# An mLSTM's running maxima: the DMAs that write and broadcast them are issued by GpSimd instead of ScalarE

## The chip, the cores and the metric

The kernel runs on one core of a Trainium2 chip. The metric is the device time of one execution in microseconds (us). The engines are TensorE (PE in the profile, its weight loads PEld), VectorE (DVE), ScalarE (ACT), GpSimd (POOL) and SyncE (SP). Each engine runs its own queue of instructions in order; a queue can hold DMA issues as well as computations, and an instruction that waits for a semaphore holds everything behind it in its queue.

## The reference

A two-layer decoder trunk for one sequence of 256 tokens, width 1024. Every layer is a half-step SwiGLU feed-forward, a token mixer beside four memory cross-attention heads, and a second half-step feed-forward. Layer 0 mixes tokens by an mLSTM (4 heads, head width 128 for keys, 256 for values), layer 1 by sliding-window attention. What matters here is the mLSTM's stabiliser. With `b` the running sum of the log forget gates and `i` the input gate,

```
b = jnp.cumsum(fc, axis=-1)
log_d = b[..., :, None] - b[..., None, :] + ic[..., None, :]
m_t = jnp.maximum(m_inter, jnp.max(log_d, axis=-1))
s = jnp.einsum('bhjd,bhsd->bhjs', qc, kc) * jnp.exp(log_d - m_t[..., None])
```

The kernel does this for all 256 tokens at once: with a[s] = i[s] - b[s] and g[t] = max over s up to t of a[s] (and 0), the weight of key s for query t is exp(a[s] - g[t]) under the causal mask. The running maxima g form 4 rows (heads) of 256 values. They are needed as rows that are the same on all 128 partitions, because keys lie on the partitions and queries along the free dimension.

## The kernel before, in words

Activations are kept transposed (features on partitions). Every weight tile of 128 x 1024 numbers is loaded by a DMA on SyncE's queue (tile `wr`, 5 buffers, L218), rounded on ScalarE to a high part (`wh`, 8 buffers, L211) and its rest formed on VectorE (`wl`, 8 buffers, L212); three matmuls per tile (L225 to L227) give nearly full precision. The rest goes through 8 PSUM banks.

The order of TensorE's and SyncE's instructions is fixed by a small planner (class `Weave`, L61): the main program yields after each group of matmuls, side chains (generators) are spawned with a delay, and each `yield` of a side chain says after how many estimated microseconds its next part may be placed. ScalarE, VectorE and GpSimd get their order from a scheduler that may move instructions.

In the mLSTM layer (`mixer_a`, L660) the gate columns are computed with the first query group of the cross-attention (L692 to L703). Then, side by side:

- `gates` (L711) transposes the gates to 4 rows (L714), forms log-sigmoids on ScalarE and VectorE (L716 to L723), runs the sum as a scan (L724), a = i - b (L725), the running maximum as a scan (`gg`, L726), b + g (L727) and its exp (`em`, L728, recorded at the helper's line L132). It then writes `gg` to a small HBM tensor `gd` (L729) and reads it back twice (L731), two heads at a time, each copy broadcast to all 128 partitions into a tile `gb[i]` of 128 x 512 numbers. TensorE's transposes of `av` and `em` into the columns `acol` (L736, L737) follow after a delay.
- `cross_spawn` (L579) normalises query rows (`head_norm`, with a power on GpSimd, L385), transposes them (L236), copies them with a gain to SBUF on ScalarE (L587, recorded at L132, input `bank,gqk`), and then each head does its scores (L599, recorded at L231), maxima (L602), exp (L605), reciprocal (L606) and normalisation (L607).
- `scores` (L747) uses `gb` first: VectorE subtracts the broadcast row from the mask (L752, L753), ScalarE takes exp with `acol` as bias, VectorE multiplies with the key-query products (L760).

Several helpers record all their operations at one line: matmuls of plain products at L231, transposes at L236, activations at L132.

Of the kernel before, what the change touches and what calls it, by code (L numbers as in the profile page):

```python
# [19 lines left out]
P = 128  # L20
# [78 lines left out]
def tile_trunk(ctx: ExitStack, tc: tile.TileContext, a, out):  # L99
    nc = tc.nc  # L100
# [30 lines left out]
    def act(*args, **kw):  # L131
        ins = nc.scalar.activation(*args, **kw)  # L132
        if args[2] not in (AF.Copy, AF.Square):
            tabled[0] = ins
# [6 lines left out]
    def unit(dt):  # L141
        return mk(up, [P, 2, T], dt, "u")
# [7 lines left out]
    def mo():  # L150
        return mk(pb8, [P, 512], F32, "bank")
# [82 lines left out]
    def transpose(ps, src):  # L234
        k = src.shape[0]
        nc.tensor.transpose(ps, src, ident[:k, :k])  # L236
        wv.now += 0.107
# [422 lines left out]
    def mixer_a(x, nxt):  # L660
# [44 lines left out]
        ipre, fpre, ab, bc, av, gg, em, one = (gt[i // 2][0:4, i % 2] for i in range(8))  # L705
        gd = a["gd"]
        gb = [unit(F32) for _ in range(2)]
# [3 lines left out]
        def gates():  # L711
            ps = mo()
            for h in range(2):
                transpose(ps[:36, h * P:(h + 1) * P], gts[:, h])  # L714
            nc.vector.memset(one, 1.0)
            nc.scalar.copy(ipre, ps[0:4, :T])  # L716
            nc.scalar.copy(fpre, ps[32:36, :T])
            nc.vector.tensor_scalar(ipre, ipre, gbias[:, 0:1], None, op0=ALU.add)
            nc.vector.tensor_scalar(fpre, fpre, gbias[:, 1:2], None, op0=ALU.add)
            nc.vector.scalar_tensor_tensor(out=ab, in0=fpre, scalar=-1.0, in1=fpre, op0=ALU.mult, op1=ALU.max)  # L720
            act(ab, ab, AF.Exp, scale=-1.0)
            act(ab, ab, AF.Ln, bias=1.0)
            nc.vector.scalar_tensor_tensor(out=fpre, in0=fpre, scalar=0.0, in1=ab, op0=ALU.min, op1=ALU.subtract)  # L723
            nc.vector.tensor_tensor_scan(bc, one, fpre, 0.0, ALU.mult, ALU.add)  # L724
            tt(out=av, in0=ipre, in1=bc, op=ALU.subtract)  # L725
            nc.vector.tensor_tensor_scan(gg, one, av, 0.0, ALU.mult, ALU.max)  # L726
            tt(out=em, in0=bc, in1=gg, op=ALU.add)  # L727
            act(em, em, AF.Exp, scale=-1.0)  # L728
            nc.scalar.dma_start(gd, gg)  # L729
            for i in range(2):  # L730
                nc.scalar.dma_start(gb[i], gd[2 * i:2 * i + 2, :].partition_broadcast(P))  # L731
            yield LAT['gates']
            pc = mo()
            for i, r in enumerate((av, em)):
                for h in range(2):
                    transpose(pc[:, (2 * i + h) * 4:(2 * i + h) * 4 + 4], r[:, h * P:(h + 1) * P])  # L736
            nc.vector.tensor_copy(acol, pc[:, :16])  # L737
            gated.append(True)

        wv.spawn(gates(), LAT['gate'])  # L740
        hsc = head_scales(x.rc, P, True)
        cross_spawn([p[:, 8:264] for p in gps], 0, 0, hsc, ys)
# [299 lines left out]
```

## Time and profile before

| | |
|---|---|
| time, median of 3 runs | 1015.86 us (1015.59 to 1018.35) |
| the profiled execution | 1016.86 us |
| its span, first to last instruction | 1015.1 us |
| mean granted TensorE clock | 0.997 |
| DMAs issued by ScalarE around 260 us | 3: `gd` at 259.07, the broadcasts from 261.26 |
| GpSimd, busy | 33.7 us, 3% of the span |

The page lists busy time per engine, a strip of 40 slices of the span (each about 25.4 us), the DMA queues, the chain of work that ended last, and the costliest groups. The views quoted below have these columns: the chain gives start, length, and what ran; a timeline gives start, length, engine, line, operation, output<-input, shapes and count, and in brackets the idle time before it with what ended that idle time; stretches give the busy time and count of PE, PEld, DVE, ACT and POOL, then the granted TensorE clock, the DMA share and GB/s. ACTq and POOLq are DMA issues of that engine's queue.

### The profile page before, as it was taken

How to read it: one execution, taken by the hardware profiler on the slowest of the kernel's cores; microseconds unless marked ns; L12 is line 12 of the kernel's file. 1: busy time of each engine (PE TensorE's matmuls, PEld its weight loads, DVE VectorE, ACT ScalarE, POOL GpSimd, SP SyncE). 2: the span in 40 equal slices, each digit the busy share in tenths (PEclk: the TensorE clock that was granted, in tenths of full speed). 3: DMA queues.
4: the chain of work that ended last, by engine and by line, in shares of the span. 5: the costliest groups of instructions: out<-in, count | busy, mean ns of one | idle time of the engine just before them, and what ended most of it. 6: DMA issues, size and time to landing. Idle time of an engine off the chain costs nothing.

```text
span 1015.1 us, 20581 instructions
## 1 busy us (share of the span) xinstructions
PE 999.3 (98%) x8572; PEld 980.4 (97%) x8572; DVE 653.7 (64%) x1060; ACT 520.1 (51%) x766; POOL 33.7 (3%) x32
## 2 busy tenths in 40 slices
PE   8999999999899999999999999999999999999998
PEld 7999999999799999999999999999987899999998
DVE  6866665566656676666567666656787766665551
ACT  7754545446466454444455544545557654444440
POOL 1200000001000000000000000000121000000000
PEclk9999999999899999999999999999999999999999
DMA  9776555666434566655566565566532246655550
GB/s 308 245 245 197 189 188 180 192 195 200 136 132 136 181 187 194 200 189 174 191 209 195 191 201 192 170 201 194 183 129 81 90 139 212 200 191 181 193 168 21
DMA packets 172180, 182.70 MB, mean 180 GB/s; under 512 B 6100, under 2 KB 167304, under 8 KB 172088
## 3 DMA queue, kind: packets, MB, share of 16 engines
q1 hardware_dynamic: 170848, 179.60, 55.5%
q10 hardware_dynamic: 1016, 1.58, 0.5%
q8 instruction: 67, 1.10, 0.4%
q0 software_dynamic: 224, 0.22, 0.2%
q14 instruction: 25, 0.20, 0.1%
HBM read 180.32 MB, written 1.05 MB: 179 GB/s over the span
## 4 chain that ended last, share of the span: by engine, by line
PE 91%; DVE 4%; ACT 2%; DMA 1%; POOL 1%; issue 1%; SPq 0%; ACTq 0%; DVEq 0%; POOLq 0%
PE bank L225 29%; PE bank L226 29%; PE bank L227 29%; PE bank L231 2%; ACT u L132 1%; DVE wl L212 1%; PE bank L236 1%; POOL col L385 1%; DMA wr<-in_mem_w_kv_dram 1%; DVE u L961 0%; DVE col L945 0%; PE bank L976 0%; DVE u L394 0%; DMA gd_dram<-u 0%; ACT wh L211 0%
## 5 line engine op out<-in xcount | busy, mean ns | idle before, releaser
L212 DVE TENSOR_TENSOR wl<-wr,wh 128x1024 fp32r<-128x1024 f32 (+1 forms) x348 | 414.7, 1193 | 281.9 <-ACT wh L211 281.3
L211 ACT CAST wh<-wr 128x1024 fp32r<-128x1024 f32 (+1 forms) x348 | 357.2, 1028 | 393.4 <-PE bank L226 369.2
L225 PE MATMUL bank<-xh,wh 128*128 128x256 f32 x1536 | 427.5, 278 | 0.0
L226 PE MATMUL bank<-xl,wh 128*128 128x256 f32 x1536 | 425.1, 277 | 0.0
L227 PE MATMUL bank<-xh,wl 128*128 128x256 f32 x1536 | 425.1, 277 | 0.0
L226 PEld LDWEIGHTS bank<-xl,wh 128*128 128x128 f32 x1536 | 289.3, 188 | 0.2
L225 PEld LDWEIGHTS bank<-xh,wh 128*128 128x128 f32 x1536 | 289.0, 188 | 0.2
L227 PEld LDWEIGHTS bank<-xh,wl 128*128 128x128 f32 x1536 | 288.9, 188 | 0.0
L225 PE MATMUL bank<-u,wh 128*128 128x256 f32 x896 | 249.3, 278 | 0.0
L226 PE MATMUL bank<-u,wh 128*128 128x256 f32 x896 | 247.6, 276 | 0.0
L227 PE MATMUL bank<-u,wl 128*128 128x256 f32 x896 | 247.6, 276 | 0.0
L225 PEld LDWEIGHTS bank<-u,wh 128*128 128x128 f32 x896 | 168.2, 188 | 1.9 <-issue 1.7
L226 PEld LDWEIGHTS bank<-u,wh 128*128 128x128 f32 x896 | 168.3, 188 | 0.1
L227 PEld LDWEIGHTS bank<-u,wl 128*128 128x128 f32 x896 | 168.2, 188 | 0.0
L225 PE MATMUL bank<-wh,xh 128*128 128x256 f32 (+1 forms) x208 | 60.0, 288 | 0.0
L226 PE MATMUL bank<-wl,xh 128*128 128x256 f32 (+1 forms) x208 | 58.1, 279 | 0.0
L227 PE MATMUL bank<-wh,xl 128*128 128x256 f32 (+1 forms) x208 | 58.0, 279 | 0.0
L487 DVE TENSOR_TENSOR t<-bank,rb 128x256 f32<-128x256 f32 x88 | 36.6, 420 | 7.3 <-PE bank L227 7.3
L225 PEld LDWEIGHTS bank<-wh,xh 128*128 128x128 f32 x208 | 39.1, 188 | 0.5 <-issue 0.3
L226 PEld LDWEIGHTS bank<-wl,xh 128*128 128x128 f32 x208 | 39.1, 188 | 0.1
L227 PEld LDWEIGHTS bank<-wh,xl 128*128 128x128 f32 x208 | 39.0, 187 | 0.0
L490 DVE TENSOR_TENSOR t<-t,bank 128x256 f32<-128x256 f32 x88 | 32.7, 412 | 1.8 <-ACT t L132 1.8
(167 smaller groups left out, 656.7 us busy)
## 6 DMA issues: line engine op xcount, KB each, us to landing
wr<-in_ffn_w_in_dram SPq DMA_DIRECT2D x176, 512.0 KB, 3.4
wr<-in_ffn_w_out_dram SPq DMA_DIRECT2D x80, 512.0 KB, 3.4
wr<-in_a_w_in_dram SPq DMA_DIRECT2D x26, 512.0 KB, 3.6
wr<-in_b_w_in_dram SPq DMA_DIRECT2D x14, 512.0 KB, 4.5
wr<-in_a_w_out_dram SPq DMA_DIRECT2D x12, 512.0 KB, 3.2
wr<-in_b_w_out_dram SPq DMA_DIRECT2D x12, 512.0 KB, 3.2
wr<-in_ffn_w_out_dram SPq DMA_DIRECT2D x16, 256.0 KB, 2.6
wr<-in_mem_w_kv_dram SPq DMA_DIRECT2D x7, 512.0 KB, 8.0
```

The costliest lines, as they stand in the source:

```text
L132: ins = nc.scalar.activation(*args, **kw)
L211: last[0] = nc.scalar.copy(hi[:, i * n:(i + 1) * n], src[:, i * n:(i + 1) * n])
L212: tt(out=lo[:, i * n:(i + 1) * n], in0=src[:, i * n:(i + 1) * n], in1=hi[:, i * n:(i + 1) * n].bitcast(F32), op=ALU.subtract)
L225: nc.tensor.matmul(ps, wh, xh, start=start, stop=False, skip_group_check=True)
L226: nc.tensor.matmul(ps, wh, xl, start=False, stop=False, skip_group_check=True)
L227: nc.tensor.matmul(ps, wl, xh, start=False, stop=stop, skip_group_check=True)
L231: nc.tensor.matmul(ps, lhsT, rhs, start=start, stop=stop, skip_group_check=True)
L236: nc.tensor.transpose(ps, src, ident[:k, :k])
L385: nc.gpsimd.tensor_tensor(out=u[:, 8:8 + 2 * n], in0=u[:, 0:2 * n], in1=mhalf[:, 0:2 * n], op=ALU.pow)
L487: tt(out=t[:, m], in0=ps[m][:, :T], in1=x.rb, op=ALU.mult)
L490: tt(out=t[:, m], in0=t[:, m], in1=ps[m][:, T:], op=ALU.mult)
```

## The change

The three DMAs of `gates` are issued from GpSimd's queue; nothing else in the source differs.

```diff
             tt(out=em, in0=bc, in1=gg, op=ALU.add)
             act(em, em, AF.Exp, scale=-1.0)
-            nc.scalar.dma_start(gd, gg)
+            nc.gpsimd.dma_start(gd, gg)
             for i in range(2):
-                nc.scalar.dma_start(gb[i], gd[2 * i:2 * i + 2, :].partition_broadcast(P))
+                nc.gpsimd.dma_start(gb[i], gd[2 * i:2 * i + 2, :].partition_broadcast(P))
             yield LAT['gates']
```

In the resulting queues they stand on GpSimd behind the second power of the cross-attention's query norm (L385) and ahead of the first power of the mLSTM's output norm (L251). On VectorE the scheduler puts the normalisation of the second query group (L394) and the scaling of the mLSTM's queries (L769) ahead of one weight split (L212), and the copy of `acol` (L737) ahead of a reciprocal (L606). TensorE's and SyncE's queues are unchanged.

## The prediction

> **What bounds the kernel now.** I read the page first, for the engine that fills the span.
>
> ```profile
> span 1015.1 us, 20581 instructions
> PE 999.3 (98%) x8572; PEld 980.4 (97%) x8572; DVE 653.7 (64%) x1060; ACT 520.1 (51%) x766; POOL 33.7 (3%) x32
> PEclk9999999999899999999999999999999999999999
> ```
>
> TensorE is busy for 98% of the span, so only time in which it stands still, or runs slowly, can be won. The clock row has one slice below 9, the eleventh, 254 to 279 us: that is where the changed DMAs are. Next I read the chain of waits there (start, length, what).
>
> ```profile
> 257.90 0.69 DVE u L726
> 259.07 2.17 DMA gd_dram<-u
> 261.26 0.36 ACTq L731
> 261.65 0.45 ACTq L731
> 262.14 0.70 ACT u L132
> 262.88 2.08 PE bank L231 x4
> 264.96 0.21 PE bank L225
> ...
> 267.52 1.37 PE bank L236 x8
> 268.89 1.09 PE bank L231 x4
> 269.98 0.12 PE bank L225
> ...
> 271.24 0.12 PE bank L227
> ```
>
> The scan (L726) makes the maxima; their write to HBM is on the chain for 2.17 us, then the two broadcast issues, and only then ScalarE's copy of the cross-attention queries (L132, tile u), for which TensorE waits. The timelines of ScalarE and TensorE say why: a queue runs in order.
>
> ```profile
> 252.14 1.04 ACT L211 CAST wh<-wr 128x1024 fp32r<-128x1024 f32 x1
> 253.09 0.41 ACT L132 ACTIVATE u<-u 4x256 f32<-4x256 f32 x1
> 253.40 1.04 ACT L211 CAST wh<-wr 128x1024 fp32r<-128x1024 f32 x1
> 259.07 0.42 ACT L132 ACTIVATE u<-u 4x256 f32<-4x256 f32 x1 [2.26 <-DVE u L727]
> 259.07 0.52 ACTq L729 DMA_DIRECT2D gd_dram<-u  x1
> 259.69 1.04 ACT L211 CAST wh<-wr 128x1024 fp32r<-128x1024 f32 x1 [0.21 <-issue]
> 261.26 0.83 ACTq L731 DMA_DIRECT2D u<-gd_dram  x2
> 262.14 0.69 ACT L132 ACTIVATE u<-bank,gqk 128x512 f32<-128x512 f32 x1 [1.40 <-DMA gd_dram<-u]
> 258.74 0.28 PE L227 MATMUL bank<-xh,wl 128*128 128x256 f32 x1
> 262.88 2.08 PE L231 MATMUL bank<-kT,u 128*128 128x256 f32 x4 [3.87 <-ACT u L132]
> ```
>
> The broadcasts cannot be issued before the write has landed, and everything behind them on ScalarE stands: 1.40 us idle ahead of the query copy, and TensorE idle for 3.87 us, from 259.02 (258.74 + 0.28) to 262.88. After that its matmuls come every 0.21 us instead of 0.12 us until about 269. The view of stretches gives the granted clock, third column from the right:
>
> ```profile
> 262.00:263.00 1.00, 0.12 (x1) 0.12 (x1) 1.00 (x3) 0.69 (x1) 0.00 (x0) 0.54 1.06 374
> 268.00:269.00 1.00, 1.00 (x7) 0.68 (x6) 0.07 (x1) 0.59 (x1) 0.00 (x0) 0.54 0.00 0
> 258.67:262.08 3.41, 0.35 (x4) 0.15 (x2) 2.81 (x4) 1.46 (x2) 0.00 (x0) 1.00 0.70 189
> 1009.60:1013.02 3.42, 1.64 (x15) 1.44 (x13) 0.85 (x2) 0.00 (x0) 0.00 (x0) 1.00 0.00 0
> ```
>
> A mean of 0.54 between full and 0.50 puts the fall at 262.08 and the return at 268.92. So the stall is paid twice: as a gap, and as 6.84 us at half clock.
>
> **The change part by part.** Durations are from the profiled execution, 1016.86 us with a span of 1015.1; it lies 1.00 above the median of 1015.86, within the runs' 1015.59 to 1018.35.
>
> *Gap.* The order of the queues shows that the three DMAs, and no other, leave ScalarE's queue; TensorE's and SyncE's order is the same. ScalarE's exp of em still waits for L727 and starts at 259.07. The cast follows 0.31 later (253.40 - 253.09), at 259.38: at 259.69 only the DMA issue is named ahead of it, and its destination buffer is read last by the matmul that ends at 259.02. The query copy follows 0.95 after it (253.09 - 252.14), at 260.33, runs 0.70 and hands over in 0.04 (262.14 + 0.70 to 262.88): TensorE restarts at 261.07. That removes 262.88 - 261.07 = **1.81 us**; a gap of 2.05 stays, now held by the chain of scans behind which em waits on ScalarE.
>
> *Clock.* If the clock stays full, the work of 262.88 to 268.89 shrinks: the scores from 2.08 to 1.09 (0.99 saved), twelve matmuls from 2.56 (264.96 to 267.52) to 1.37 (269.98 to 271.35, twelve of about 0.114) (1.19 saved), the eight transposes by the same ratio from 1.37 to 0.73 (0.64 saved): **2.82 us**. Will it stay full? I cut the trace into stretches of 3.41 us, half the slow spell, counted from the fall at 262.08. The stretch before the fall was 10% busy (0.35 of 3.41). A stretch 48% busy (1.64 of 3.42) was followed by no fall. A gap of 2.05 leaves a stretch at least 40% busy, whatever the cut. I take no fall.
>
> The Trainium skill, "TensorE: Matmul & The Clock Gate", Part 1, puts this down to a free-running window of 3413 ns, and the 6.84 us seen are two of them. The same part says that the clock falls after at least one idle window; in this trace a stretch 10% busy was enough, so the row decides. Its closing table asks for no idle gaps over about 3 us, by which a gap of 2.05 keeps the clock.
>
> *What is late next.* The second query pair: its transposes end at 261.07 + 1.09 + 1.37 + half of 0.73 = 263.9, ScalarE's copy (0.69) at 264.6, and TensorE needs it after the other half, 1.09 of scores and twelve more matmuls, at 266.7. Later producers are fed by TensorE itself and keep their distance to it. DVE's order changes in three places (two PSUM reads go ahead of a weight split, the copy of acol ahead of a reciprocal). The split is for a tile used some 200 matmuls later. The reciprocal is held until the transposes end at 264.3, its product (0.69) is there by 265.2, and TensorE reads it after 266.7 and 24 matmuls of 0.114, past 269.4. Both cost nothing; without that cover they would cost below 1 us each.
>
> *The DMAs on GpSimd.* Rows of its timeline, and of the issues (last number: us to landing):
>
> ```profile
> 49.25 0.61 POOL L183 DMA_DIRECT2D u<-in_mask_dram  x1
> 307.52 0.69 POOL L251 TENSOR_TENSOR col<-col,mhalf 128x2 f32<-128x2 f32 x1 [53.66 <-DVE col L250]
> u<-gd_dram ACTq DMA_DIRECT2D x2, 256.0 KB, 5.4
> u<-in_mask_dram POOLq DMA_DIRECT2D x1, 192.0 KB, 6.1
> gblk<-in_b_k_norm_g_dram POOLq DMA_DIRECT2D x1, 8.0 KB, 6.6
> 48.91 1.23 DVE L212 TENSOR_TENSOR wl<-wr,wh 128x1024 fp32r<-128x1024 f32 x1 [0.39 <-ACT wh L211]
> 277.78 0.41 DVE L752 TENSOR_TENSOR u<-con,u 128x256 f32<-128x256 f32 x1
> 279.15 0.69 DVE L607 TENSOR_TENSOR u<-u,col 128x512 f32<-128x512 f32 x1
> 285.10 0.60 PE L236 MATMUL bank<-con,u 128*128 128x128 f32 x4
> ```
>
> GpSimd's queue is empty for 53.66 us up to 307.52, so the stall moves to a queue in which nothing waits behind it: cost nothing, unless the broadcasts are late. Their first reader is L752 at 277.78, about 4.6 us earlier after the change: 273.2. The maxima are there at 258.6. At the fast end the two steps take what they took on ScalarE, 2.17 and 5.4: landing at 266.2. At the slow end each takes the slowest landing of a GpSimd issue, 6.6, and the second broadcast is issued another 0.61 later: 271.8 and 272.4. Both ends are ahead of 273.2, and I take the middle, about 269. If they were late, DVE would wait at L752, and TensorE first for what follows it: the probabilities of L607 (279.84), transposed at 285.10, a further cover of about 5.3 us. So they cost TensorE nothing up to a landing at 278.5.
>
> The Trainium skill, "SBUF — State Buffer", section "SBUF: two separate sides", speaks against this move: GpSimd writes its descriptors through a port that it shares with DVE, and is locked out while DVE runs a two-port operation, so such DMAs are better issued from ScalarE or SyncE. Here the mask's issue at 49.25 lay inside a DVE split (48.91 to 50.14) and took 0.61, so that DVE operation did not hold it; the only DVE work near these issues is of this kind or reads PSUM. If each of three issues were held for a whole split, an estimate of 3 x 1.23 = 3.7 us later, the landing at 276.1 would still be under that cover.
>
> *Sum.* 1.81 + 2.82 = 4.63 us off 1016.86: **1012.2 us**, 0.36% below the median of 1015.86. If the profile's 1.00 over the median belongs to the profiling, it is 1011.2.
>
> **The rivals.**
>
> *The clock falls all the same.* The limit lies somewhere between 10% and 48% busy; evenly spread, it is above 40% in one case of five, and the 2.05 us must then fall nearly whole into one stretch, about two cases of five. Price: one or two stretches at half clock, 1.7 to 3.4 us, so 1013.9 to 1015.6. For it: the limit is not shown. Against: the clock row has one low slice only.
>
> *Part of the gain is met by another wait.* If ScalarE's cast and copy follow less closely than 0.31 and 0.95, or the faster TensorE meets DVE's next results early, 1 to 2 us come back: 1013.2 to 1014.2. For it: DVE is near full between 258 and 263. Against: those results are fed by TensorE itself.
>
> *Slower: the broadcasts land late.* Place: L752 on DVE, which holds the probabilities of the cross heads and the score banks behind it. It decides from a landing at 278.5, 19.9 us after the scan; the whole gain is gone at 283.1, and it is slower by 0.3% (3.05 us) from 286.2, 27.6 us after the scan, more than twice the slow end. A landing at 290 gives 1012.2 + 11.5 = 1023.7. Only the untried size, 256 KB with one source row for all partitions on GpSimd's queue, speaks for it; the 192 KB mask is the nearest.
>
> *The change doesn't do what it says.* If something else held the query copy until 262.1, the time would stay near 1016. The cast ahead of it has no other open wait, so this is small.
>
> **How the numbers follow.** Forecast 0.75 (1011 to 1013), clock falls 0.09 (1013.9 to 1015.6), another wait 0.09 (1013.2 to 1014.2), late broadcasts 0.04, no effect 0.03. The range, 1010.8 to 1014.4, takes the forecast with the profile's offset, the other wait and the cheap end of the clock's fall. About 0.3%, 3.05 us, is what a measurement of this kernel can tell from no change: faster means below 1012.8. Within the forecast 1012.2 is only 0.6 from that, and I give it five cases in six, 0.63; same gets 0.33, slower 0.04.
>
> **What would show it.** Right: no DMA issue on ScalarE near 259; the query copy at about 260.3; TensorE's gap near 2.05; no clock value under 0.9 between 250 and 280; three issues on GpSimd from about 258.6, landed before L752, with no DVE wait there. Wrong: half clock after the gap (first rival), a gap near 3 or new TensorE waits before 290 (second), DVE idle ahead of L752 for more than 5 us (third). Another execution may cut the stretches elsewhere; then the kernel before would pay another clock loss than the 2.82 here, and the difference of the two would be smaller, while the time after stays.

## The result and the profile after

| | before | after |
|---|---|---|
| median of 16 runs each | 1015.99 us (1015.47 to 1018.35) | 1014.14 us (1012.48 to 1016.43) |
| ratio | | 0.9979, 95% interval 0.9970 to 0.9987 |
| the profiled execution | 1016.86 us | 1014.12 us |
| its span | 1015.1 us | 1012.3 us |

The change makes the kernel 0.2% faster, 1.85 us in the medians. The runs after lie in three groups: five from 1012.48 to 1012.80, whose mean granted clock is 1.000; seven from 1013.69 to 1014.24 at 0.998; four from 1015.69 to 1016.43 at 0.996 to 0.997. The forecast of 1012.2 is the first group, and the median is in the second. The profiled execution belongs to the second group; no run of the third was profiled.

The page of after: TensorE busy for 99% instead of 98%, and the clock row no longer shows its low slice, since a slice of 25 us hides a short fall.

```profile
span 1012.3 us, 20586 instructions
PE 998.1 (99%) x8572; PEld 979.3 (97%) x8572; DVE 653.9 (65%) x1060; ACT 520.0 (51%) x766; POOL 35.5 (4%) x35
PEclk9999999999999999999999999999999999999999
```

The chain of waits of after at the same place, which answers to the second fence of the prediction:

```profile
257.87 0.69 DVE u L726
258.58 0.42 DVE u L727
...
259.35 1.03 ACT wh L211
260.38 0.59 ACT u L132
260.97 0.04 issue
261.02 1.14 PE bank L231 x4
262.16 0.21 PE bank L225
...
264.72 1.18 PE bank L236 x8
265.90 1.06 PE bank L231 x4
```

The DMAs are gone from it: after the scans come em's exp (259.03), one weight cast and the query copy, back to back. But the matmuls behind the restart still come every 0.21 us, up to about 265. The timelines of after, ScalarE, TensorE, GpSimd, and VectorE's first reader of the broadcasts:

```profile
259.03 0.42 ACT L132 ACTIVATE u<-u 4x256 f32<-4x256 f32 x1 [2.26 <-DVE u L727]
259.35 1.03 ACT L211 CAST wh<-wr 128x1024 fp32r<-128x1024 f32 x1
260.29 0.68 ACT L132 ACTIVATE u<-bank,gqk 128x512 f32<-128x512 f32 x1
261.02 1.14 PE L231 MATMUL bank<-kT,u 128*128 128x256 f32 x4 [2.04 <-ACT u L132]
258.84 0.58 POOL L729 DMA_DIRECT2D gd_dram<-u  x1 [5.01 <-DVE u L726]
261.85 1.10 POOL L731 DMA_DIRECT2D u<-gd_dram  x2 [2.43 <-DMA gd_dram<-u]
274.72 0.42 DVE L752 TENSOR_TENSOR u<-con,u 128x256 f32<-128x256 f32 x1
```

The query copy starts at 260.29 (forecast 260.33), TensorE restarts at 261.02 (261.07) after 2.04 us (2.05). GpSimd waits 2.43 us for the write, with nothing behind it. The two broadcasts are issued from 261.85 and land 4.6 and 5.3 us after their issues, by about 267.7, some 7 us ahead of L752, which waits for nothing.

The view of stretches of after, third column from the right the clock; the two of 1 us place the fall and the return:

```profile
262.00:263.00 1.00, 1.00 (x6) 1.00 (x5) 1.00 (x2) 0.00 (x0) 0.96 (x2) 0.50 1.00 346
265.00:266.00 1.00, 1.00 (x8) 0.66 (x7) 0.06 (x1) 0.40 (x1) 0.00 (x0) 0.79 0.83 275
258.59:262.00 3.41, 1.37 (x9) 1.07 (x8) 3.41 (x6) 1.93 (x3) 0.73 (x2) 1.00 0.74 184
```

The clock fell at 262.00 and came back at 265.42 (0.79 between 0.50 and 1), so one spell of 3.42 us instead of the 6.84 of before. The stretch of 3.41 us that ended at the fall was 40% busy (1.37 of 3.41). This execution pays 3.42 / 2 = 1.7 us for it.

### The profile page after: what moved, and what is told of

Same layout as the page of the kernel before. It is cut to its first block, busy times and chain, and to the rows that moved or that the text cites. A ratio compares the mean times of both kernels' runs of the same rounds, so it can differ in the third digit from the quotient of the medians.

```text
span 1012.3 us, 20586 instructions
## 1 busy us (share of the span) xinstructions
PE 998.1 (99%) x8572; PEld 979.3 (97%) x8572; DVE 653.9 (65%) x1060; ACT 520.0 (51%) x766; POOL 35.5 (4%) x35
## 4 chain that ended last, share of the span: by engine, by line
PE 90%; DVE 5%; ACT 2%; POOL 1%; issue 1%; DMA 1%; SPq 0%; ACTq 0%; DVEq 0%; POOLq 0%
PE bank L225 29%; PE bank L226 29%; PE bank L227 29%; PE bank L231 2%; DVE wl L212 1%; ACT u L132 1%; POOL col L385 1%; PE bank L236 1%; DMA wr<-in_mem_w_kv_dram 1%; ACT wh L211 0%; DVE u L961 0%; DVE col L945 0%; PE bank L976 0%; DVE col L380 0%; DVE u L394 0%
## 5 line engine op out<-in xcount | busy, mean ns | idle before, releaser
L212 DVE TENSOR_TENSOR wl<-wr,wh 128x1024 fp32r<-128x1024 f32 (+1 forms) x348 | 414.9, 1194 | 280.8 <-ACT wh L211 280.2
```

Source lines behind the costliest of these rows:

```text
L212: tt(out=lo[:, i * n:(i + 1) * n], in0=src[:, i * n:(i + 1) * n], in1=hi[:, i * n:(i + 1) * n].bitcast(F32), op=ALU.subtract)
```

## The experiments

Theory: the kernel pays two separate prices at this place, the time for which TensorE stands still, and a fall of the clock that the standstill causes in some executions, by where it lies in fixed stretches of 3.41 us. The change shortened the first by 1.83 us (3.87 to 2.04) and left the second in most runs. Rivals: the groups come from the DMAs themselves; another wait took the place of the one removed; GpSimd's queue makes the broadcasts late.

### The gap filled: after with 16 and with 4 matmuls, before with 32

```diff
             s = mo()
+            if layer == 0 and gi == 0 and m == 0:
+                for _ in range(16):
+                    nc.tensor.matmul(s[:, :T], identb, maskb[:, :T], start=True, stop=True, skip_group_check=True)
             for h in range(2):
                 mmf(s[:, h * T:(h + 1) * T], qT[:, m, h * P:(h + 1) * P], kT[gi][:, m], T)
```

> The changed kernel with 16 small matmuls (bf16, 128x256, results overwritten at once) put on TensorE into the gap ahead of the first cross-attention scores. They need no other engine and take about 16 x 0.11 = 1.8 us of the 2.04 us gap, so the scores start when they did. Clock theory: the slow runs of the changed kernel pay 1.7 us or 3.4 us only because the gap lowers the granted clock; with the gap filled the clock stays at 1.000 in every run and all times lie at 1012.5 (1012.3 to 1012.9), with no clusters at 1014.1 and 1015.8. Rival (the difference between runs comes from the DMAs or from when the broadcasts land, and the clock only goes with it): the clusters stay, median near 1014.1.

> The kernel before with 32 such matmuls in its gap of 3.87 us (about 3.5 us of it). It keeps the ScalarE stall and takes the clock loss away, so it measures the first term of the sum alone. Clock theory: clock 1.000 in all runs, time 1012.5 + 1.81 = 1014.3 (1014.1 to 1014.6), that is some 1.7 us below the median of before. Rival (the half clock is no separate cost): no change from 1016.0.

> The changed kernel with 4 filler matmuls only, about 0.44 us, so that TensorE stands still for 1.6 us instead of 2.04. It asks where the limit lies: stretches of 3.41 us that were 10% and 40% busy were followed by half clock, one 48% busy was not. With 1.6 us idle no stretch is under 53% busy. Clock theory with a limit between 40% and 48%: full clock in all runs, 1012.5. Rival (any standstill above about 1.5 us can lower the clock): clusters at 1012.5 and 1014.2 remain.

Measured: with 16 on after, 1012.50 us, ratio to before 0.9962 (0.9949 to 0.9974), four of five runs at 1012.29 to 1012.51, one at 1014.09 with a mean clock of 0.998. With 32 on before, 1014.31 us, 0.9982 (0.9973 to 0.9991); eight of eleven runs at 1013.72 to 1014.40 with a clock of 0.999 or 1.000, three at 1015.86 to 1016.34 with 0.998. With 4 on after, 1012.44 us, 0.9958 (0.9945 to 0.9972), all five runs at 1012.29 to 1012.54. The idle times that were left, one timeline row of TensorE for each, first 16, then 32, then 4:

```profile
261.07 1.13 PE L231 MATMUL bank<-kT,u 128*128 128x256 f32 x4 [0.27 <-ACT u L132]
```

```profile
262.89 1.13 PE L231 MATMUL bank<-kT,u 128*128 128x256 f32 x4 [0.70 <-ACT u L132]
```

```profile
261.14 1.13 PE L231 MATMUL bank<-kT,u 128*128 128x256 f32 x4 [1.58 <-ACT u L132]
```

TensorE restarts at the same times as in after and in before, so the fillers shorten nothing; they only keep the clock. That alone takes 1.6 us off the median of after (1014.14 to 1012.50; the ratios to before are 0.9979 and 0.9962), and of the ten runs with 16 and with 4 fillers one lies in a slower group, against 11 of the 16 of after. On before it takes off 2.2 us by the runs of before on the same chip (1016.53; 1.7 us by the 1015.99 above). It shows the clock loss as a price of its own, and gives the other term pure: 1014.31 - 1012.47, the middle of the other two, = **1.84 us** for the gap, forecast 1.81. The few runs at 0.998 that remain probably lost the clock elsewhere; no trace caught one, so where stays open. One place to look is 11 to 14 us, where TensorE waits twice in a row: 0.44 and 0.88 us in the trace with 16 fillers, but 0.98 and 0.87 us in that of `bcast_on_act` (below), together 1.85 us. No trace shows a fall there.

### Two fillers: where the limit lies

> The changed kernel with two filler matmuls, so that TensorE stands still for about 1.8 us, between the 2.04 us that lowered the clock in most runs and the 1.58 us that lowered it in none of five. A stretch of 3.41 us is then at least 47% busy. Theory (limit between 40% and 48% busy): full clock in nearly all runs, 1012.45; at most a few runs near 1014.1 if the limit is close to 47%. Rival (the limit is nearer to 54%, what four fillers left): about as many runs at 1014.1 as in the changed kernel.

```diff
-                for _ in range(4):
+                for _ in range(2):
```

Measured: twelve runs, median 1013.50 us, ratio 0.9976 (0.9961 to 0.9991): six at 1012.29 to 1012.81, three at 1014.18 to 1014.25, two at 1015.19 and 1015.70, and one at 1020.43, which nothing here explains. The profiled execution is one of the first group, and the whole standstill (1.79 us) lay in one of its stretches:

```profile
258.78:262.19 3.41, 1.62 (x11) 1.20 (x10) 3.41 (x6) 1.93 (x3) 0.58 (x1) 1.00 0.71 182
262.19:265.61 3.42, 3.42 (x28) 3.13 (x27) 2.06 (x6) 1.60 (x5) 1.10 (x2) 1.00 0.73 192
```

The places of the stretches come from other falls in the same trace, for within an execution they keep their step. With five broadcasts (`bcast_x5`, below) the clock falls at 261.40, at 281.88 and, behind the last matmul, at 1019.16: 20.48 and 757.76 us after the first, which is 6 and 222 steps of 3.4133 us. In this trace the fall behind the last matmul is at 1009.71, 220 steps after 258.78.

At 48% busy (1.62 of 3.41) no fall followed, as at the end of the kernel before. With five broadcasts a stretch 41% busy (1.41 of 3.42, 278.46 to 281.88) was followed by half clock, like the 40% of after. So the traces hold the limit between 41% and 48%. That five more runs lost clock all the same speaks for a limit close to 48%, or for falls elsewhere; the runs don't tell these apart.

That the cut decides is seen in the two kernels with repeated broadcasts, in both of which TensorE stands still here for 2.03 us. With five, one stretch (257.98 to 261.40) holds the whole standstill, is 41% busy (1.39 of 3.42), and the clock falls. With four (`bcast_x4`) the standstill lies across two stretches, 55% and 85% busy, and the clock stays:

```profile
257.29:260.71 3.42, 1.89 (x17) 1.69 (x15) 3.35 (x6) 1.49 (x3) 0.58 (x1) 1.00 0.89 271
260.71:264.12 3.41, 2.91 (x20) 2.64 (x21) 2.61 (x5) 1.22 (x4) 1.10 (x2) 1.00 0.74 195
```

### Which of the three DMAs held ScalarE

> Half of the change: the write of the maxima stays on ScalarE, the two broadcasts go to GpSimd. Theory: what holds ScalarE is the wait of the broadcasts for the landed write; the write itself costs only its issue, some 0.3 us ahead of the query copy (in the trace of before the cast behind the issue starts at 259.69 instead of 259.35). TensorE restarts near 261.4, the runs at full clock lie near 1012.8, the others 1.7 or 3.4 us higher, so a median near 1014.5. Rival (the write on ScalarE is the costly one): as before, near 1016.3.

> The other half: the write goes to GpSimd, the broadcasts stay on ScalarE, where they wait for it (the first weight cast then stands behind the query copy). Theory: the write lands 2.5 us after its issue at 258.84, at 261.3; two issues of 0.4 follow, the query copy runs from 262.2 and TensorE restarts near 262.9, as before: near 1014.4 at full clock, median near 1016.3. Rival: as the changed kernel, 1014.1.

In after.py, `nc.scalar.dma_start(gd, gg)` for the first, `nc.scalar.dma_start(gb[i], ...)` for the second. Measured: with the write alone on ScalarE 1014.15 us, 0.9970 (0.9957 to 0.9983); with the broadcasts alone on it 1017.18 us, 1.0002 (0.9991 to 1.0013). ScalarE's timeline, first with the write, then with the broadcasts:

```profile
259.01 0.51 ACTq L729 DMA_DIRECT2D gd_dram<-u  x1
259.63 1.04 ACT L211 CAST wh<-wr 128x1024 fp32r<-128x1024 f32 x1 [0.21 <-issue]
260.58 0.68 ACT L132 ACTIVATE u<-bank,gqk 128x512 f32<-128x512 f32 x1
```

```profile
262.53 0.82 ACTq L731 DMA_DIRECT2D u<-gd_dram  x2
263.41 0.69 ACT L132 ACTIVATE u<-bank,gqk 128x512 f32<-128x512 f32 x1 [3.58 <-DMA gd_dram<-u]
```

The write costs its issue: TensorE restarts at 261.31 instead of 261.02, and 0.3 us is too little to be seen in the times (1014.15 against 1014.14). The broadcasts cost the wait. With the write issued by GpSimd it took 3.3 us to land in that execution, so ScalarE stood 3.58 us, longer than the 1.40 of before, where a cast filled part of the wait; TensorE restarted at 264.15 instead of the 262.9 expected, and the time is 0.9 us above the 1016.3 expected. So the gain comes from moving the two broadcasts: moved alone they give what the change gives, and the write moved alone gives nothing.

### The query copy ahead of the wait

> The changed kernel with the rest of the gap removed at its cause: the exp of em is put behind the copy of the first cross-attention queries in ScalarE's queue, and one weight cast that reads a buffer TensorE is still using goes behind that copy too. The copy can then run at about 256.3, when its transposes end, and TensorE never waits for it. Theory: no gap and no half clock, 1012.5 - 2.0 = 1010.5 (1010.2 to 1011.2) in all runs, below both kernels. Rival (another wait takes the gap's place, such as the maxima or the exps of the first scores, since ScalarE still waits for the scans): 1011.5 to 1012.5, with a new TensorE wait shortly behind.

> The order of query_first, but all three DMAs issued by ScalarE, behind the query copy (the broadcasts fall behind the second query copy there). Theory: the engine that issues is not what counts, only what stands behind the wait in its queue; the write has landed by about 261.3, before the broadcasts' turn comes, so ScalarE hardly waits: as query_first, 1010.2 (1010.0 to 1010.8). Rival (DMAs on ScalarE cost for themselves, by issue time or by broadcasts landing late): 1011.5 or more.

```diff
+    firstq, casts = [], [0]
...
+            casts[0] += bool(firstq)
+            with tc.issue_after(firstq[0].ins) if casts[0] == 8 else ExitStack():
+                last[0] = nc.scalar.copy(hi[:, i * n:(i + 1) * n], src[:, i * n:(i + 1) * n])
...
+            ins = nc.scalar.activation(qT, ps, AF.Copy, scale=gqk[:, layer:layer + 1])
+            if not firstq:
+                firstq.append(ins)
...
-            act(em, em, AF.Exp, scale=-1.0)
             yield LAT['gates']
+            with tc.issue_after(firstq[0].ins):
+                act(em, em, AF.Exp, scale=-1.0)
```

The counter `casts` finds the one weight cast that goes behind the copy, the eighth that the source issues after it. The second kernel has the three DMAs under the same `with`, on ScalarE. Measured: 1010.22 us, ratio to before 0.9939 (0.9927 to 0.9952), with GpSimd, one of its five runs at 1011.56 with a clock of 0.998, above the range expected; 1010.40 us, 0.9934 (0.9922 to 0.9947), with ScalarE. Both beat both kernels. ScalarE and the stretch of 250 to 290 us of the first (lines are shifted by a few):

```profile
256.25 0.69 ACT L590 ACTIVATE u<-bank,gqk 128x512 f32<-128x512 f32 x1 [1.89 <-PE bank L239]
258.99 0.41 ACT L133 ACTIVATE u<-u 4x256 f32<-4x256 f32 x1 [2.05 <-DVE u L732]
```

```profile
250.00:290.00 40.00, 40.00 (x317) 38.72 (x316) 31.01 (x59) 24.41 (x49) 2.69 (x4) 1.00 0.51 156
```

The copy runs 4 us earlier, in time in which ScalarE had been waiting for the scans, and TensorE is busy for all of the 40 us at full clock. ScalarE of the second:

```profile
259.25 0.51 ACTq L736 DMA_DIRECT2D gd_dram<-u  x1
263.15 0.47 ACT L133 ACTIVATE u<-bank,col 128x256 f32<-128x256 f32 x1 [0.94 <-DVE col L607]
263.16 0.36 ACTq L738 DMA_DIRECT2D u<-gd_dram  x1
```

Here the scheduler put the first broadcast 3.9 us behind the write (and ahead of the second query copy, not behind it as expected). The row ahead of it waits for VectorE and not for the write, whose landing this trace doesn't show; the 2.17 us of before would have it landed by then. With the order mended the issuing engine makes no difference that these runs show. The rival, a new wait in the place of the old, is refuted for this stretch.

### Late broadcasts

> The changed kernel with each broadcast done five times in a row into the same tile, each waiting for the one before; every turn takes about 4.9 us from issue to landing, so the last of the first tile lands near 287 instead of 267. It tests the rival in which late broadcasts make the kernel slower. Theory: the first reader (L752 on VectorE, at 274.7 in the trace of after) then waits, but TensorE has a cover of 5.3 us behind that, up to about 280: the kernel gets slower by the 7 us beyond it, to near 1021 (1018 to 1023), and TensorE shows a wait of that length at the transposes of the cross-attention probabilities, shortly after 280. Rival (VectorE's stall is made up elsewhere): below 1016.

> The changed kernel with each broadcast done four times in a row. With five the last one landed at 283.7, 8.9 us after VectorE was ready for it, and TensorE lost 5.9 us, so the cover was 3.0 us and not 5.3. With four the last should land near 278.5, 3.6 us late. Corrected cover of 3.0 us (ScalarE's exps of the score weights wait for the rows, and the copy of the transposed cross-attention probabilities stands behind them): TensorE waits about 0.6 us ahead of the cross-attention value products. Cover of 5.3 us as in the prediction: no new TensorE wait.

```diff
-            for i in range(2):
-                nc.gpsimd.dma_start(gb[i], gd[2 * i:2 * i + 2, :].partition_broadcast(P))
+            for _ in range(5):
+                for i in range(2):
+                    nc.gpsimd.dma_start(gb[i], gd[2 * i:2 * i + 2, :].partition_broadcast(P))
```

Measured: five, 1023.66 us, ratio 1.0064 (1.0049 to 1.0080), a little above the 1018 to 1023 expected; four, one run of 1019.86 us. VectorE, ScalarE and TensorE with five:

```profile
283.71 0.42 DVE L753 TENSOR_TENSOR u<-con,u 128x256 f32<-128x256 f32 x1 [8.85 <-DMA u<-gd_dram]
284.17 0.80 ACT L132 ACTIVATE u<-u,acol 128x256 f32<-128x256 f32 x2 [8.26 <-DVE u L753]
285.13 0.58 ACT L614 COPY t<-bank 128x512 f32<-128x512 f32 x1
285.76 2.08 PE L231 MATMUL bank<-t,vM 128*128 128x256 f32 x4 [5.89 <-ACT t L614]
```

And with four, VectorE and TensorE:

```profile
279.97 0.42 DVE L753 TENSOR_TENSOR u<-con,u 128x256 f32<-128x256 f32 x1 [6.54 <-DMA u<-gd_dram]
282.03 2.08 PE L231 MATMUL bank<-t,vM 128*128 128x256 f32 x4 [3.59 <-ACT t L614]
```

8.85 - 5.89 = 2.96 and 6.54 - 3.59 = 2.95: the cover behind VectorE's wait is 3.0 us in both, not 5.3. TensorE is held not by the probabilities' transposes but by ScalarE: its exp of the score weights waits for the rows, and the copy of the transposed probabilities (L614) stands behind it. The 0.6 us expected for four came out as 3.59 because the last broadcast was used at 279.97 instead of 278.5, and because TensorE, with its clock kept at the first gap, brought VectorE to L753 at 273.4 already. With five the last broadcast lands earlier than expected (283.7, not 287) and the time is longer all the same: TensorE has less cover, and the clock is at half for 3.41 us from 261.40 and for 6.82 us from 281.88, a mean of 0.994 in the profiled run.

## Why the prediction was right, and where it was wrong

The time came out at 1014.14 us, inside the range of 1010.8 to 1014.4 and near its upper end; the likeliest time, 1012.2, was 1.9 us too low, and the forecast of a gain over 0.3%, at 0.63, didn't come: the gain is 0.21%. That the median lies in the range is luck in part: the mechanism forecast, full clock after the gap, gives 1012.5 and holds in five of 16 runs, and the range reached 1014.4 only because it took in the cheap end of the first rival.

- *Gap.* Right, step by step: the copy at 260.29 against 260.33, the restart at 261.02 against 261.07, 1.84 us by the filled kernels against 1.81.
- *Clock.* This step failed. "A gap of 2.05 leaves a stretch at least 40% busy, whatever the cut. I take no fall." The stretch was 40% busy in the trace of after, and the clock fell: 3.42 us at half clock, 1.7 us, stand where its sum put nothing. The rows of before left the limit open between 10% and 48%, and I spread it evenly; it lies between 41% and 48%, at the very end. The first rival, given 0.09 and a price of 1.7 to 3.4 us, is what happened in most runs: 11 of 16 lie above 1013.6, with a clock below 1.000. The price was about right: the second and third groups lie 1.6 and 3.3 us above the first. A limit close to 48% would let about half of all cuts lower the clock (estimated from 2.04 us of standstill, of which 1.8 must fall into one stretch of 3.41), so 11 of 16 may hold some falls from elsewhere, as in the filled kernels.
- *The same term of before.* 2.82 us was read from one execution. Over its 16 runs before loses 1015.99 - 1014.31 = 1.7 us in the median, and after 1014.14 - 1012.5 = 1.6. So in the medians the clock loss hardly changed, and nearly all of their difference of 1.85 us is the gap. (The filled kernels were timed apart from these 16 runs, beside runs of before that lost 2.2; the five runs of after at clock 1.000, 1012.48 to 1012.80, agree with the filled ones.) The last sentence of the prediction allowed for another loss of before and a smaller difference; that the time after stays was wrong.
- *The skill's rules.* The Trainium skill, "TensorE: Matmul & The Clock Gate", Part 1, speaks of an idle window; the stretch of after that was 40% busy was followed by half clock. Its section "Why this matters for your kernels" warns of gaps over about 3 us; 2.04 us was already too long in the trace of after. The measurements decide against both.
- *What is late next, and the sum of the rest.* Right: no new wait for TensorE. The row of after with the larger times (transposes at 264.72) only shows the half clock.
- *The DMAs on GpSimd.* Right: 2.5 us for the write and about 4.9 for the broadcasts, there by about 267.7, between the two ends of 266.2 and 271.8. The three issues took 0.54 to 0.58 us beside VectorE's splits, so nothing of a lockout is seen in them.
- *The slower rival.* Its mechanism exists, but its point was wrong: the cover is 3.0 us and not 5.3, because I followed VectorE's queue behind the wait and not ScalarE's. It stayed without effect, since the broadcasts came 7 us early.
- *The change doesn't do what it says.* Refuted: ScalarE's wait is gone.

## What to carry to other kernels

Where a DMA must wait for another DMA, look at what stands behind it in its queue: here the remedy was to put the one copy that TensorE needs ahead of the wait, and then it no longer mattered which engine issues the DMA. Price a standstill of TensorE twice, as time and as clock, and ask how long it is against the 3.41 us stretches: 1.6 us cost no clock in five runs, 2.0 us cost 1.6 us or more in most. A clock loss read from one trace is one draw: the same kernel's runs differ by one or two spells of 1.7 us.

## What the runs showed of the hardware that was not expected

The fall needs no idle stretch: 41% busy was too little, 48% enough. In the seven falls that the traces show between matmuls, a spell lasted one stretch (3.42 us) where TensorE was back before the fall (after, `write_on_act`, the first of `bcast_x5`) and two (6.84 us) where it was not (before, `bcast_on_act`, `bcast_x4`, the second of `bcast_x5`). The kernel before was 77% busy in the stretch after the fall, and the clock stayed low for another:

```profile
262.08:265.49 3.41, 2.61 (x8) 2.25 (x9) 1.68 (x4) 0.69 (x1) 0.00 (x0) 0.50 0.85 254
```

The four runs of after's third group lost as much as one spell of two stretches, or two of one; without a trace of them this stays open.

A few bf16 matmuls into a bank that is overwritten next keep the clock: four of them, under half a microsecond of work, took 1.7 us off the median of after.
